# A seven-product unit for one more value/gate column group, its two raw-weight additions done by accumulating transfers

## The chip, the cores and the metric

One Trainium2 chip, one core. The metric is the device time of one execution in microseconds (us), the median of several runs; the profile is one further execution on the same core. PE is TensorE (PEld its weight load), DVE is VectorE, ACT is ScalarE, POOL is GpSimd, SP is SyncE, which issues most loads.

## The reference

Two layers on 256 tokens of width 2048 in float32: a gated linear attention (GLA) layer with 4 heads, then a retention layer with 8 heads, each with a residual add, and a final RMSNorm. Of the GLA layer:

```python
proj = h @ w_in                       # q, k, v, gate
log_a = jax.nn.log_sigmoid(((h @ w_a1) @ w_a2 + b_a)) / 16.0
scores = jnp.einsum('bhtk,bhsk,bhtsk->bhts', qb, kb, decay)   # causal, chunked with a state
o = o * lax.rsqrt(jnp.mean(o * o, axis=-1, keepdims=True) + EPS)
return (o.reshape(B, S, D_INNER) * head_g * jax.nn.silu(gate)) @ w_out
```

A GLA head has 256 key columns and 1024 value columns; the kernel treats its values and gates as two column groups of 512, so head 1 has groups g2 and g3.

## The kernel before

**Precision.** Every large product of float32 matrices is three matmuls of rounded halves: high x high, high x low, low x high. The token side lies split in SBUF (`xhl` for the layer's input, `ogt` for the mixer's output, both transposed). The weight side is split on the way: a *step* is a block of 256 x 512 weights (512 KB). SP loads it into one of eight `raw` buffers, ACT writes its high half `hi` (L298), DVE its low half `lo` (L299), PE multiplies. `hi_p` and `lo_p` have four buffers each, so a step's `hi` can be written when PE has used up a step four places or so before; `LOOK = 3` steps are split ahead.

**Groups and units.** A plain group of 512 output columns is eight steps of 12 matmuls for its values (`gv`, `group_x`) and eight for its gates (`gg`): 192 matmuls. Some pairs of groups are done as a *unit* (`values_and_gates` for heads, `out_pair` for the output projection): the first half of the contraction, as a 2 x 2 block product of tokens by columns, takes seven products of 12 matmuls (P1 to P8 without P4; each product has two steps of 6) in place of eight, and the second half is eight direct steps (v4 to v7, g4 to g7): 84 + 96 = 180 matmuls. A unit needs sums of token blocks (`make_sums`, four tiles, on DVE and ACT) and sums of weight blocks. The latter are made in the `raw` buffers: transfers from DRAM that add to what is there (`accum_op`, issued by POOL, L310), and for P6 two additions of one raw buffer to another on DVE (L293), written in `EARLY = 2` steps ahead. `UNIT` is the order of the steps. `JOINT` lists the units: of the GLA heads only g5 and g7, of the GLA output projection both pairs of its first half (`gae`).

**Head 1.** After its q/k group (`gqk`) come, in the program, the side work of that head, taken up a piece at a time between steps: the decays (`lc`), seven levels of masked scores (`w`, matmuls `lv` of 128 x 128), their masking on DVE (`m`, L819 and L821), fourteen small additions on POOL (`s`, L828), and the split into `sc` (ACT L722, DVE L723). `o_part` multiplies `sc` by the values (`go_ps`); `og_part` normalises (the chain `hm`, `hr_nw`, `hr` of two-element DVE instructions), scales by the gate `gsg`, transposes on PE (`got_tp`) and writes `ogt` (ACT L499, DVE L500). The gate's SiLU, `gsg` (L686), empties the PSUM banks of the gate group.

**Order.** A scheduler fixes each engine's order at build time; every engine then works its list in that order. PSUM has four accumulator banks (`acc`, handed out in turn by `slots`); g3's gates follow g2's in banks that `gsg` of g2 must empty. `rs` is a pool of one 16 KB buffer per partition: first the residual `resid`, loaded at the start, later the token sums `xsum`. Token sums for g5 and g7 (`xsum`) are made during head 2; those for the output pairs (`osum`) during g3.

Of the kernel before, what the change touches and what calls it, by code (L numbers as in the profile page):

```python
# [17 lines left out]
P = 128  # L18
SEQ = 256
D = 2048  # L20
# [44 lines left out]
def _plan():  # L65


    loads, subs = [], []

    def load(gid, j):  # L70
        loads.append((gid, j))
        return len(loads) - 1

    def use(c, pre=None, post=()):
        subs.append((c, pre, post))

    def plain(gid, js=range(NSUB)):
        for j in js:
            use(load(gid, j))

    def pair(g, v, q=None, order=None):
        order = (order or UNIT).split()
        x = [load(g, 0), load(g, 1)] if order[0] == "P1" else []
        z = []
        later = max(("P3", "P6"), key=order.index)
        for n, tok in enumerate(order):
            kind, i = tok[0], tok[1:]
            if kind in "qvg":
                plain({"q": q, "v": v, "g": g}[kind], [int(i)])
            elif tok == "z":  # L90
                z += [load(v, 2), load(v, 3)]
            elif tok == "P2":
                plain(g, [2, 3])
            else:
                if tok == "P1" and not x:
                    x += [load(g, 0), load(g, 1)]
                for j in range(2):
                    post = []
                    if tok == later:
                        post.append((z[j], (v, j)))  # L100
                    if tok == "P1":
                        post.append((x[j], (v, j)))
                    if tok == "P6":
                        post.append((x[j], (g, 2 + j)))
                    use(z[j] if tok in ("P3", "P7") else x[j], z[j] if tok == "P6" else None, post)

    def out_cols_of(name, half, cut, joint):
        for c in (0, 2):
            cols = [(name, half, c + n) for n in range(2)]
            if joint[c // 2]:  # L110
                pair(cols[1], cols[0])
                continue
# [36 lines left out]
    buf = []  # L149
    for c in range(len(loads)):  # L150
        b = min([*range(NRAW), *_spare(loads[c])], key=lambda n: free[n])
        buf.append(b)
        free[b] = last[c]
    return loads, subs, places, last, buf


UNIT = "P1 v4 z P3 v5 P5 v6 P6 P2 v7 P7 g4 g5 P8 g6 g7"
MIXED = "q0 q1 P1 q2 q3 q4 z P5 q5 P6 q6 q7 P2 P3 v4 v5 v6 P7 v7 g4 g5 P8 g6 g7"
WHOLE = " ".join(f"q{j}" for j in range(NSUB)) + " " + UNIT


def ret_order(h):
# [4 lines left out]
HEAD = 4  # L167
EARLY = 2
JOINT = {
    "a": (5, 7),  # L170
    ("ao", 0): (True, True),
    ("ao", 1): (False, True),
    ("ro", 0): (False, True),
# [5 lines left out]
def kernel(  # L179
# [104 lines left out]
    def emit_split(pieces=1, between=None):  # L284
        i = emitted["sub"]
        c, pre, post = subs[i]
        emit_raws(c)
        src = raws[c]
        for n in range(i + 1, min(i + 1 + EARLY, len(subs))):
            at, by = subs[n][:2]  # L290
            if by is not None and n not in added:
                added.add(n)
                nc.vector.tensor_tensor(raws[at], raws[at], raws[by], ALU.add)  # L293
        hi, lo = split_tiles(i)
        step = SUB // pieces
        for k in range(pieces):
            sl = slice(k * step, (k + 1) * step)
            a = nc.scalar.activation(hi[:, sl], src[:, sl], AF.Copy)  # L298
            b = nc.vector.tensor_tensor(lo[:, sl], src[:, sl], hi[:, sl].bitcast(F32), ALU.subtract)  # L299
            if i >= last0 - 4:  # L300
                keep(a)
                keep(b)
            if i == 0:
                first(a, b)
                if k == 0:
                    between()
        splits[i] = (hi, lo)
        emitted["sub"] += 1
        for n, key in post:
            nc.gpsimd.dma_start(raws[n], block(key), accum_op=ALU.add)  # L310
        emit_raws(c)
# [125 lines left out]
    def sums_in_v(name):  # L437
        return lambda n: v_p.tile([P, 2, QK, 2, P], F32R, tag="v", name=f"{name}{n}")

    def make_sums(lhs, name, where):  # L440
        s = cur["s"] = [None] * 4
        room = where(name)
        tt = nc.vector.tensor_tensor
        y = [t4_p.tile([P, QK, SEQ], F32, tag="t4", name=f"{name}_y{i}") for i in range(2)]
# [33 lines left out]
    def get_resid(name):  # L478
        r = rs_p.tile([P, 2, D], F32, tag="rs", name=name)
        nc.gpsimd.dma_start(r, cur["resid_at"])  # L480
        cur["resid"] = r

    def put_resid(name):
        at = dram_p.tile([P, 2, D], F32, tag=name, name=name)
        nc.scalar.dma_start(at, cur["resid"])
# [17 lines left out]

    sm = const([P, 96], "smalls")[:, 0:S_N]
    ident = const([P, P], "ident")
    cur["resid"] = rs_p.tile([P, 2, D], F32, tag="rs", name="resid")
    xhl = const([P, NKT, 2, SEQ], "xhl", F32R)
    ogt = const([P, NKT, 2, SEQ], "ogt", F32R)
    trig = const([P, 2, SEQ], "trig")
# [84 lines left out]
        nc.vector.tensor_scalar(m, ss, 1.0 / D, EPS, ALU.mult, ALU.add)  # L594
        rsqrt(r[:, 0, ts], m, n, name)

    def square_sum(t, c):
        junk = sg_p.tile([P, GW], F32, tag="sg", name="sqj")
        return nc.scalar.activation(
            junk, cur["resid"][:, t, c * GW : (c + 1) * GW], AF.Square, accum_out=ssum[:, t, c : c + 1]  # L600
        )

    zs = sc_p.tile([80, SEQ], F32R, tag="dm", name="zs", bufs=1)
# [38 lines left out]
                make_xhl(kt)  # L642

    def gate_low_rank():
        for t in range(2):
            keep(nc.sync.dma_start(cur["resid"][:, t, :], x_n[:, t, :]))
            yield
        nc.gpsimd.dma_start(mask_t, mask_in)
        for c in range(8):
            square_sum(c // 4, c % 4)  # L650
            if c % 2:
                yield
        token_norm(rr, "n1")
# [181 lines left out]
    def gla_head(h):  # L835
# [70 lines left out]
        def joint_turn(tok):  # L906
            if tok == "v4":
                o_part(0)
            elif tok == "g5":
                o_part(1)  # L910
            else:
                advance()

        for gi in range(2):
# [14 lines left out]
            def v_hook(j):  # L929
                if h > 0 and gi == 1 and j == 1:  # L930
                    o_part(0)
                if h == 1 and gi == 1 and j > 1:
                    if j == 2:
                        cur["making"] = make_sums(ogt, "osum", sums_in_v)
                    if j < 6:
                        next(cur["making"])

            def g_hook(j):
                if h == 0 and gi == 1 and j == 5:
                    o_part(0)  # L940
                if gi == 1 and j == (6 if h == 0 else 2):
                    o_part(1)
                if gi == 1 and h == 1 and j == 3:
                    next(cur["making"])

            if h == 0 and gi == 1:
                drain_side()
                side.append(scores())
            if h == 2 and gi == 0:
                side.append(make_sums(xhl, "xsum", sums_in_rs))  # L950
            pv = group_x(xhl, f"gv{g}", v_hook)
            vs.append(v_evac(pv, r2, f"gv{g}"))
            sgs.append(g_evac(group_x(xhl, f"gg{g}", g_hook), r, f"gsg{g}"))
# [20 lines left out]
            f"xt2_{c}",  # L974
        )

    def out_pair(c, first, name, final=False):
        lhs, s = ogt, cur["s"]
        B, A, C, V1 = acc(4, f"{name}e{c}_ps", which=list(slots))
        slots.rotate(-2)  # L980
# [34 lines left out]
        cur["pin"] = final  # L1015
        product(A, plain(0, 0), stop=True)
        advance()
        direct(lhs, (C, V1), 4)
        join(g, 0, A)
        advance()  # L1020
        product(C, summed(0))
        advance()
        direct(lhs, (C, V1), 5)
        drain_side()
        product(P5, summed(1), stop=True)
        direct(lhs, (C, V1), 6)
        for t in range(2):
            join(c, t, P5)
        product(A, summed(2), stop=True)
        product(B, plain(4, 0))  # L1030
        join(c, 0, A, ALU.subtract)
        direct(lhs, (C, V1), 7, stop=True)
# [55 lines left out]
    def out_half(first, final, name, cut=0, hook=None, joint=(False, False)):  # L1088
        pend = {}
        for c in range(4):  # L1090
            if joint[c // 2]:
                if c % 2 == 0:
                    out_pair(c, first, name)
                continue
            if cut and c == 0:
                if True:
# [346 lines left out]

    for h in range(2):
        gla_head(h)
    slots = deque((2, 3, 0, 1))
    out_half(True, False, "ga", joint=JOINT["ao", 0])
    slots = deque((2, 3, 0, 1))
    put_resid("resid_x")
    for h in range(2, 4):  # L1450
        gla_head(h)
    get_resid("gb_resid")
# [125 lines left out]
```

## Time and profile before

| | |
|---|---|
| median of 3 runs | 1374.77 us (1374.18 to 1375.06) |
| profiled execution | 1373.6 us, span 1371.8 us |
| PE busy | 1361.9 us (99%) |
| DVE, ACT, POOL busy | 1100.0 (80%), 846.6 (62%), 136.7 us (10%) |
| granted TensorE clock | 0.998 |
| DMA | 315.03 MB, mean 230 GB/s |

The times are those of one execution each; the rows of the profile belong to one that took 1373.6 us, of which 1371.8 us lie between its first and last instruction. A row of the order in time begins with start and duration in us.

### The profile page before, as it was taken

How to read it: one execution, taken by the hardware profiler on the slowest of the kernel's cores; microseconds unless marked ns; L12 is line 12 of the kernel's file. 1: busy time of each engine (PE TensorE's matmuls, PEld its weight loads, DVE VectorE, ACT ScalarE, POOL GpSimd, SP SyncE). 2: the span in 40 equal slices, each digit the busy share in tenths (PEclk: the TensorE clock that was granted, in tenths of full speed). 3: DMA queues.
4: the chain of work that ended last, by engine and by line, in shares of the span. 5: the costliest groups of instructions: out<-in, count | busy, mean ns of one | idle time of the engine just before them, and what ended most of it. 6: DMA issues, size and time to landing. Idle time of an engine off the chain costs nothing.

```text
span 1371.8 us, 18375 instructions
## 1 busy us (share of the span) xinstructions
PE 1361.9 (99%) x6564; PEld 1143.5 (83%) x6564; DVE 1100.0 (80%) x1524; ACT 846.6 (62%) x1116; POOL 136.7 (10%) x194
## 2 busy tenths in 40 slices
PE   9999999999999999999999999999999999999997
PEld 8888888888888888888888888888888888888886
DVE  7686795987878896769888888887867897889796
ACT  6576656656567747656666566655546666666565
POOL 1003020110021021001011010100101101010010
PEclk9999999999999999999999999999999999999999
DMA  9755566789658667868897878896798797869773
GB/s 365 257 172 167 174 203 184 158 249 324 192 153 268 205 205 180 314 168 239 271 321 201 256 202 252 207 313 215 174 363 230 234 262 195 262 194 321 236 179 121
DMA packets 84507, 315.03 MB, mean 230 GB/s; under 512 B 9776, under 2 KB 10800, under 8 KB 83136
## 3 DMA queue, kind: packets, MB, share of 16 engines
q1 hardware_dynamic: 67200, 241.63, 50.6%
q0 software_dynamic: 15920, 64.89, 23.7%
q10 hardware_dynamic: 1296, 7.35, 1.5%
q8 instruction: 51, 0.84, 0.2%
q14 instruction: 40, 0.33, 0.1%
HBM read 303.35 MB, written 10.49 MB: 229 GB/s over the span
## 4 chain that ended last, share of the span: by engine, by line
PE 96%; DMA 2%; DVE 1%; issue 1%; ACT 0%; DVEq 0%; POOL 0%; ACTq 0%; POOLq 0%
PE rqk_ps L383 8%; PE re_ps L412 7%; PE re_ps L413 7%; PE re_ps L411 7%; PE rqk_ps L384 4%; PE gqk_ps L383 4%; PE gg_ps L341 3%; PE gv_ps L342 3%; PE gv_ps L341 3%; PE gv_ps L340 3%; PE gg_ps L342 3%; PE gg_ps L340 3%; PE ge_ps L413 2%; PE ge_ps L411 2%; PE ge_ps L412 2%; PE gae_ps L413 2%
## 5 line engine op out<-in xcount | busy, mean ns | idle before, releaser
L299 DVE TENSOR_TENSOR lo<-raw,hi 128x1024 fp32r<-128x1024 f32 (+1 forms) x568 | 687.1, 1219 | 215.6 <-ACT hi L298 206.5
L298 ACT ACTIVATE hi<-raw 128x1024 fp32r<-128x1024 f32 (+1 forms) x568 | 596.1, 1055 | 393.8 <-PE gg_ps L342 49.0
L383 PE MATMUL rqk_ps<-xhl,hi 128*128 128x512 f32 x480 | 162.8, 397 | 0.0
L412 PE MATMUL re_ps<-lo,xhl 128*128 128x512 f32 x352 | 137.4, 390 | 0.3 <-DVE lo L299 0.3
L413 PE MATMUL re_ps<-hi,xhl 128*128 128x512 f32 x352 | 137.1, 390 | 0.0
L310 POOL DMA_DIRECT2D raw<-in_w_all x90 | 78.0, 868 | 555.4 <-DVE lo L299 270.6
L411 PE MATMUL re_ps<-hi,xhl 128*128 128x512 f32 x352 | 132.4, 391 | 0.0
L384 PE MATMUL rqk_ps<-xhl,lo 128*128 128x256 f32 x480 | 122.3, 280 | 0.0
L383 PEld LDWEIGHTS rqk_ps<-xhl,hi 128*128 128x128 f32 x480 | 89.5, 188 | 17.9
L384 PEld LDWEIGHTS rqk_ps<-xhl,lo 128*128 128x128 f32 x480 | 87.5, 189 | 3.4
L412 PEld LDWEIGHTS re_ps<-lo,xhl 128*128 128x128 f32 x352 | 66.1, 188 | 13.9 <-DVE lo L299 0.8
L413 PEld LDWEIGHTS re_ps<-hi,xhl 128*128 128x128 f32 x352 | 66.1, 188 | 13.7
L411 PEld LDWEIGHTS re_ps<-hi,xhl 128*128 128x128 f32 x352 | 66.0, 188 | 13.3
L383 PE MATMUL gqk_ps<-xhl,hi 128*128 128x512 f32 x216 | 76.6, 399 | 0.0
L341 PE MATMUL gg_ps<-lo,xhl 128*128 128x512 f32 x192 | 75.4, 393 | 0.0
L341 PE MATMUL gv_ps<-lo,xhl 128*128 128x512 f32 x192 | 75.2, 392 | 0.0
L340 PE MATMUL gv_ps<-hi,xhl 128*128 128x512 f32 x192 | 75.1, 393 | 0.0
L342 PE MATMUL gv_ps<-hi,xhl 128*128 128x512 f32 x192 | 75.0, 391 | 0.0
L342 PE MATMUL gg_ps<-hi,xhl 128*128 128x512 f32 x192 | 74.9, 390 | 0.0
L340 PE MATMUL gg_ps<-hi,xhl 128*128 128x512 f32 x192 | 74.8, 391 | 0.0
L828 POOL TENSOR_TENSOR s<-s,m 128x64 f32<-128x64 f32 x56 | 36.0, 674 | 232.6 <-DVE m L819 223.3
L384 PE MATMUL gqk_ps<-xhl,lo 128*128 128x256 f32 x216 | 59.0, 280 | 0.0
(434 smaller groups left out, 2654.8 us busy)
## 6 DMA issues: line engine op xcount, KB each, us to landing
raw<-in_w_all SPq DMA_DIRECT2D x449, 512.0 KB, 5.0
raw<-in_w_all POOLq DMA_DIRECT2D x90, 512.0 KB, 6.9
resid<-in_x_n SPq DMA_DIRECT2D x2, 1024.0 KB, 10.0
gg<-in_gn_g POOLq DMA_DIRECT2D x8, 256.0 KB, 4.4
resid_x<-resid ACTq DMA_DIRECT2D x1, 2048.0 KB, 7.9
gb<-in_gn_b POOLq DMA_DIRECT2D x8, 256.0 KB, 5.8
gb_resid<-resid_x POOLq DMA_DIRECT2D x1, 2048.0 KB, 11.1
resid_g<-gb_resid ACTq DMA_DIRECT2D x1, 2048.0 KB, 9.5
```

What stands on the lines that cost most here:

```text
L298: a = nc.scalar.activation(hi[:, sl], src[:, sl], AF.Copy)
L299: b = nc.vector.tensor_tensor(lo[:, sl], src[:, sl], hi[:, sl].bitcast(F32), ALU.subtract)
L310: nc.gpsimd.dma_start(raws[n], block(key), accum_op=ALU.add)
L340: pin(mm(ps, xh, hi[:, q, :], start=kt == begin, stop=False))
L341: pin(mm(ps, xh, lo[:, q, :], start=False, stop=False))
L342: pin(mm(ps, xl, hi[:, q, :], start=False, stop=kt == end - 1))
L383: mm(ps[c], wh, rhs[:, kt, :, :], start=kt == 0, stop=False)
L384: mm(ps[c][:, 0, :], wl, rhs[:, kt, 0, :], start=False, stop=False)
L411: pin(mm(ps, xh, hi[:, q, :], start=start, stop=False, **again))
L412: pin(mm(ps, xh, lo[:, q, :], start=False, stop=False, **again))
L413: pin(mm(ps, xl, hi[:, q, :], start=False, stop=stop, **again))
L828: nc.gpsimd.tensor_tensor(dst, dst, side_of(m[:, li, :], z), ALU.add)
```

## The change

Group g3 becomes a unit too, with the order `UNIT`. Its matmuls go from 192 to 180, its steps from 16 to 22, and it needs six more accumulating loads. What comes with it:

- The two raw-weight additions for its P6 are transfers from one SBUF buffer to another with `accum_op`, issued by POOL; all other units keep the DVE additions.
- The token sums `xsum` are made during head 1's q/k group, kept in DRAM (`keep_sums`, 2 MB) and loaded again before head 2. They lie in the one buffer of `rs`, so the input rows for the norm go into two tiles of the value pool at the start, and the residual is loaded (`get_x`, 2 MB by POOL) after g3's last use of the sums.
- `osum` is made at five places of g3's unit, into `cur["os"]`.
- The first output pair (`gae`, columns 0 and 1) has a new order, `LATE` with `late_direct`: P1, P2, P3 come before the direct step v4, so the first use of g2's and g3's `ogt` is later, and the side work (`og_part`) is spread over it.

```diff
@@ plan and JOINT
-                pair(cols[1], cols[0])
+                pair(cols[1], cols[0], order=LATE if cols[0] == ("ao", 0, 0) else None)
+LATE = "P1 P2 z P3 v4 P5 v5 P6 v6 v7 P7 g4 g5 P8 g6 g7"
-    "a": (5, 7),
+    "a": (3, 5, 7),
@@ emit_split
-                nc.vector.tensor_tensor(raws[at], raws[at], raws[by], ALU.add)
+                if loads[at][0] == ("ag", 3):
+                    nc.gpsimd.dma_start(raws[at], raws[by], accum_op=ALU.add)
+                else:
+                    nc.vector.tensor_tensor(raws[at], raws[at], raws[by], ALU.add)
@@ new
+    def get_x():
+        cur["resid"] = rs_p.tile([P, 2, D], F32, tag="rs", name="resid")
+        for t in range(2):
+            nc.gpsimd.dma_start(cur["resid"][:, t, :], x_n[:, t, :])
@@ gate_low_rank
-            keep(nc.sync.dma_start(cur["resid"][:, t, :], x_n[:, t, :]))
+            xs.append(v_p.tile([P, D], F32, tag="v", name=f"x_n{t}"))
+            keep(nc.sync.dma_start(xs[t], x_n[:, t, :]))
@@ gla_head
             if tok == "v4":
                 o_part(0)
+                if h == 1:
+                    cur["making"] = make_sums(ogt, "osum", sums_in_v, "os")
...
+            elif h == 1 and tok in ("P3", "v5", "P5", "P6", "P8"):
+                next(cur["making"])
...
-            if h == 2 and gi == 0:
-                side.append(make_sums(xhl, "xsum", sums_in_rs))
+            if h == 1 and gi == 0:
+                keep_sums("xsum")
@@ out_pair, first pair of the GLA output
+        if late_direct:
+            product(B, plain(4, 0))
+            join(g, 0, A)
+            advance()
+            product(C, summed(0))
+            while len(side) > 1:
+                advance()
+            advance()
+            direct(lhs, (C, V1), 4)
...
@@ program
     for h in range(2):
         gla_head(h)
+        if h == 0:
+            side.append(make_sums(xhl, "xsum", sums_in_rs))
+    get_x()
+    cur["s"] = cur["os"]
...
     put_resid("resid_x")
+    reload_sums("xsum2")
```

The scheduler moves more than the diff says. On PE, at the start of g3 before (`gv_ps`): the last scores matmul (`w_x` into `lv`) stands 43 matmuls above these rows' first `go_ps`, of which the last eight are shown.

```order
L342 MATMUL gv_ps_1946<-hi_1901,xhl 128x512
L340 MATMUL gv_ps_1947<-hi_1901,xhl 128x512
L341 MATMUL gv_ps_1947<-lo_1902,xhl 128x512
L342 MATMUL gv_ps_1947<-hi_1901,xhl 128x512
L340 MATMUL gv_ps_1946<-hi_1925,xhl 128x512
L341 MATMUL gv_ps_1946<-lo_1926,xhl 128x512
L696 MATMUL go_ps_1984<-gv_1741,sc_1850 128x512
L697 MATMUL go_ps_1984<-gv_1741,sc_1850 128x512
```

The same place of the changed kernel (`ge_ps_1973` takes P1, `ge_ps_1975` takes v4 and P3):

```order
L773 MATMUL lv_1_1641<-w_x 128x128 x2
L415 MATMUL ge_ps_1973<-hi_1924,xhl 128x512
L416 MATMUL ge_ps_1973<-lo_1925,xhl 128x512
L417 MATMUL ge_ps_1973<-hi_1924,xhl 128x512
L415 MATMUL ge_ps_1973<-hi_1924,xhl 128x512
L416 MATMUL ge_ps_1973<-lo_1925,xhl 128x512
L417 MATMUL ge_ps_1973<-hi_1924,xhl 128x512
L707 MATMUL go_ps_2016<-gv_1763,sc_1872 128x512
L708 MATMUL go_ps_2016<-gv_1763,sc_1872 128x512
L707 MATMUL go_ps_2017<-gv_1763,sc_1872 128x512
L708 MATMUL go_ps_2017<-gv_1763,sc_1872 128x512
L415 MATMUL ge_ps_1975<-hi_1947,xhl 128x512
```

Between the last scores matmul and the use of the finished scores `sc` stand six matmuls now. In all, 12 matmuls of P1 and the 8 of levels 4 to 7 stand between the start of g3 and `go_ps`; before, these 8 stood ahead of g3, and 26 matmuls of g3 ahead of `go_ps`.

On ACT, in the changed kernel (`hi_1947` to `hi_1998` are the steps v4, P3 and v5 of g3; `gg_ps` are g2's gate banks, of which `ge_ps_1975` reuses the first):

```order
L302 ACTIVATE hi_1947<-raw_1796 128x1024
L302 ACTIVATE hi_1977<-raw_1825 128x1024
L302 ACTIVATE hi_1987<-raw_1852 128x1024
L302 ACTIVATE hi_1998<-raw_1875 128x1024
L733 ACTIVATE sc_1872<-s_1_1643 128x384
L697 ACT_TABLE_LOAD
L697 ACTIVATE gsg_1967<-gg_ps_1768,rr 128x512
```

Before, the order on ACT was the same (three `hi`, `sc`, table load, `gsg`), but no product of g3's values waited for `gsg`: `gv_ps` of g3 lay in the banks that g2's values had left.

On DVE, at the first output pair. Before, the last of the chain `hr` and the scalings of `go` stand ahead of the pair's steps (`hi_2293` and `hi_2346` are steps of its P1 and of P3):

```order
L496 SCALAR_TENSOR_TENSOR hr_2228<-hr_nw 128x2
L894 SCALAR_TENSOR_TENSOR go_1995<-go_1995,hr_2228,gsg_1943 128x512 x2
L299 TENSOR_TENSOR lo_2294<-raw_2091,hi_2293 128x1024
L299 TENSOR_TENSOR lo_2320<-raw_2109,hi_2319 128x1024
L894 SCALAR_TENSOR_TENSOR go_2199<-go_2199,hr_2228,gsg_2337 128x512 x2
L299 TENSOR_TENSOR lo_2347<-raw_2134,hi_2346 128x1024
L500 SCALAR_TENSOR_TENSOR ogt<-got_tp_2282,smalls,ogt 128x256
```

In the changed kernel (`lo_2503` and `lo_2515` are the two steps of P6, `lo_2527` and `lo_2547` are v6 and v7):

```order
L303 TENSOR_TENSOR lo_2503<-raw_2143,hi_2502 128x1024
L505 SCALAR_TENSOR_TENSOR hr_2353<-hr_nw 128x2
L303 TENSOR_TENSOR lo_2515<-raw_2145,hi_2514 128x1024
L905 SCALAR_TENSOR_TENSOR go_2027<-go_2027,hr_2353,gsg_1967 128x512
L905 SCALAR_TENSOR_TENSOR go_2277<-go_2277,hr_2353,gsg_1971 128x512
L905 SCALAR_TENSOR_TENSOR go_2027<-go_2027,hr_2353,gsg_1967 128x512
L905 SCALAR_TENSOR_TENSOR go_2277<-go_2277,hr_2353,gsg_1971 128x512
L303 TENSOR_TENSOR lo_2527<-raw_2294,hi_2526 128x1024
L998 TENSOR_TENSOR resid<-gae_p_2375,resid 128x512 x2
L303 TENSOR_TENSOR lo_2547<-raw_2312,hi_2546 128x1024
L509 SCALAR_TENSOR_TENSOR ogt<-got_tp_2424,smalls,ogt 128x256
```

The chain `hm` to `hr` and the four scalings now stand between the steps P2 and P6 of the output pair. On PE the products P1, P2, P3, P5 and P6 (60 matmuls) stand ahead of the eight transposes `got_tp` of g2's output, and four matmuls of v4 follow before the first that needs a low half of `ogt`.

More of the change, by code (lines that the diff above doesn't have):

```diff
@@ L438, in sums_in_v, with make_sums @@
         return lambda n: v_p.tile([P, 2, QK, 2, P], F32R, tag="v", name=f"{name}{n}")
-    def make_sums(lhs, name, where):
-        s = cur["s"] = [None] * 4
+    def make_sums(lhs, name, where, into="s"):
+        s = cur[into] = [None] * 4
         room = where(name)
@@ L505 @@
     ident = const([P, P], "ident")
-    cur["resid"] = rs_p.tile([P, 2, D], F32, tag="rs", name="resid")
     xhl = const([P, NKT, 2, SEQ], "xhl", F32R)
@@ L595, in token_norm, with square_sum @@
         rsqrt(r[:, 0, ts], m, n, name)
-    def square_sum(t, c):
+    def square_sum(t, c, src=None):
         junk = sg_p.tile([P, GW], F32, tag="sg", name="sqj")
+        src = cur["resid"][:, t] if src is None else src
         return nc.scalar.activation(
-            junk, cur["resid"][:, t, c * GW : (c + 1) * GW], AF.Square, accum_out=ssum[:, t, c : c + 1]
+            junk, src[:, c * GW : (c + 1) * GW], AF.Square, accum_out=ssum[:, t, c : c + 1]
         )
@@ L644, in gate_low_rank @@
     def gate_low_rank():
+        xs = []
         for t in range(2):
[L646 removed]
+            xs.append(v_p.tile([P, D], F32, tag="v", name=f"x_n{t}"))
+            keep(nc.sync.dma_start(xs[t], x_n[:, t, :]))
             yield
@@ L649, in gate_low_rank @@
         for c in range(8):
-            square_sum(c // 4, c % 4)
+            square_sum(c // 4, c % 4, xs[c // 4])
             if c % 2:
@@ L931, in v_hook @@
                     o_part(0)
[L932 to L936, printed above, removed]
             def g_hook(j):
@@ L942, in g_hook @@
                     o_part(1)
-                if gi == 1 and h == 1 and j == 3:
-                    next(cur["making"])
             if h == 0 and gi == 1:
@@ L975, in out_transposes, with out_pair @@
         )
-    def out_pair(c, first, name, final=False):
+    def out_pair(c, first, name, final=False, late_direct=False):
         lhs, s = ogt, cur["s"]
@@ L1017, in out_pair @@
         advance()
[L1018 to L1032, printed above, removed]
+        if late_direct:
[7 more added lines that the diff above has]
+            direct(lhs, (C, V1), 4)
+            advance()
+            product(P5, summed(1), stop=True)
+            advance()
+            direct(lhs, (C, V1), 5)
+            for t in range(2):
+                join(c, t, P5)
+            drain_side()
+            product(A, summed(2), stop=True)
+            direct(lhs, (C, V1), 6)
+            join(c, 0, A, ALU.subtract)
+            direct(lhs, (C, V1), 7, stop=True)
+        else:
+            direct(lhs, (C, V1), 4)
+            join(g, 0, A)
+            advance()
+            product(C, summed(0))
+            advance()
+            direct(lhs, (C, V1), 5)
+            drain_side()
+            product(P5, summed(1), stop=True)
+            direct(lhs, (C, V1), 6)
+            for t in range(2):
+                join(c, t, P5)
+            product(A, summed(2), stop=True)
+            product(B, plain(4, 0))
+            join(c, 0, A, ALU.subtract)
+            direct(lhs, (C, V1), 7, stop=True)
         product(A, summed(3), stop=True)
@@ L1092, in out_half @@
                 if c % 2 == 0:
-                    out_pair(c, first, name)
+                    out_pair(c, first, name, late_direct=first and c == 0 and name == "ga")
                 continue
```

## The prediction

> **What bounds the kernel now.** I read the engine totals first, then what PE waited for, then the windows around the third to fifth column groups, then each engine's order in time there.
>
> ```profile
> span 1371.8 us, 18375 instructions
> PE 1361.9 (99%) x6564; PEld 1143.5 (83%) x6564; DVE 1100.0 (80%) x1524; ACT 846.6 (62%) x1116; POOL 136.7 (10%) x194
> ```
>
> ```profile
> PE warm_ps L520 <- POOL lnone L522: 1.0, 1, 1.0
> PE re_ps L412 <- DVE lo L299: 0.3, 1, 0.3
> PE zps L639 <- DVE wa L613: 0.3, 1, 0.3
> ```
>
> The second view is the whole list of PE's waits: 1.6 us in three places. So a matmul that goes is a gain in full, and a microsecond of a new wait is a loss in full: PE has nowhere to make it up. The question is whether the engines that feed PE keep their lead at the two places that the change reorders. The windows are q/k and values/gates of g2, g3, and the first output pair; columns are PE, PEld, DVE, ACT, POOL.
>
> ```profile
> 125.00:153.00 28.00, 28.00 (x157) 24.12 (x156) 17.20 (x33) 18.63 (x32) 0.00 (x0) 1.00 0.49 156
> 153.00:201.00 48.00, 48.00 (x236) 40.51 (x235) 40.45 (x71) 27.91 (x38) 6.83 (x11) 1.00 0.65 201
> 201.00:249.00 48.00, 48.00 (x214) 39.72 (x213) 29.99 (x43) 29.08 (x40) 3.98 (x7) 1.00 0.60 168
> 249.00:290.00 41.00, 41.00 (x190) 34.06 (x189) 36.00 (x40) 27.01 (x32) 5.17 (x6) 1.00 0.83 241
> ```
>
> DVE is at 84% in g2 and 88% in the output pair, with PE at 100%: what DVE gets there in addition comes late.
>
> **Matmuls saved.** PE's order in time at the end of g2, and from the chain the scores matmuls:
>
> ```profile
> 198.23 0.39 PE L340 MATMUL gg_ps<-hi,xhl 128*128 128x512 f32 x1
> ...
> 200.95 0.39 PE L340 MATMUL gv_ps<-hi,xhl 128*128 128x512 f32 x1
> ```
>
> ```profile
> 195.91 1.34 PE lv L762 x12
> ```
>
> Twelve matmuls lie between the starts 198.23 and 200.95: 2.72 us, 0.227 each. The unit has 180 in place of 192, so 12 x 0.227 = 2.7 us go. A small scores matmul costs 1.34/12 = 0.11.
>
> **First wait: the scores at the start of g3.** Count from g3's first matmul as zero. By the order, P1's 12 matmuls and 8 small ones come first: PE is at `go_ps` at 12 x 0.227 + 8 x 0.11 = 3.6 and, after four of them, at v4 at 4.5. Both wait for ACT: `go_ps` for `sc`, v4 for the bank that g2's `gsg` empties. What feeds them, on ACT (a step of g2, then the end of its scores), on DVE (two pieces of `w`, then a `lo` and `m`) and on POOL (the additions of head 1 in one block, and those of head 2 in two):
>
> ```profile
> 194.41 1.06 ACT L298 ACTIVATE hi<-raw 128x1024 fp32r<-128x1024 f32 x1 [2.12 <-PE gg_ps L342]
> ```
>
> ```profile
> 203.21 0.53 ACT L722 ACTIVATE sc<-s 128x384 fp32r<-128x384 f32 x1 [1.00 <-POOL s L828]
> 203.76 1.28 ACT L686 ACT_TABLE_LOAD   x1
> 205.05 1.27 ACT L686 ACTIVATE gsg<-gg_ps,rr 128x512 f32<-128x512 f32 x2
> ```
>
> ```profile
> 190.75 0.42 DVE L800 TENSOR_TENSOR w<-w,qk 128x256 f32<-128x256 f32 x1
> 191.08 0.41 DVE L801 TENSOR_TENSOR w<-w,qk 128x256 f32<-128x256 f32 x1
> ```
>
> ```profile
> 192.76 1.22 DVE L299 TENSOR_TENSOR lo<-raw,hi 128x1024 fp32r<-128x1024 f32 x1
> 193.90 0.68 DVE L819 TENSOR_TENSOR m<-lv,mask 128x512 f32<-128x512 f32 x1
> ```
>
> ```profile
> 194.73 8.45 POOL L828 TENSOR_TENSOR s<-s,m 128x64 f32<-128x64 f32 x14 [32.77 <-DVE m L819]
> ```
>
> ```profile
> 377.20 4.73 POOL L828 TENSOR_TENSOR s<-s,m 128x64 f32<-128x64 f32 x8 [69.51 <-DVE m L819]
> 386.59 3.21 POOL L828 TENSOR_TENSOR s<-s,m 128x64 f32<-128x64 f32 x6 [4.66 <-DVE m L821]
> ```
>
> Before, the additions began at 194.73, 6.2 us ahead of g3's first matmul (200.95), and `sc` had its high half at 203.74. Now `m` stands in DVE's queue behind the `lo` of P1 and of v4. The first row of ACT shows that a `hi` starts when PE has used up the step whose buffer it takes. P1's first `hi` takes that of g2's fifth gate step, used up three steps and the 8 small matmuls before the last one drains at zero: -(3 x 2.72 + 0.9) + 0.16 = -8.9 (0.16 is 0.39 less 0.23). With 1.06 and 1.22 its `lo` ends at -6.6. Behind it come 13 pieces of `w` (0.33 from start to start), a `lo` (1.14 likewise, 192.76 to 193.90), 4 pieces, the `lo` of v4, and `m`: 17 x 0.33 + 2 x 1.14 + 0.68 = 8.6, so 2.0. POOL follows 0.15 later (194.73 against 193.90 + 0.68) and takes 4.73 + 3.21 = 7.9: 10.1. From the start of `sc` to the first of two `gsg` ends 205.05 + 0.64 - 203.21 = 2.5: 12.6. PE stood ready at 4.5: **a wait of 8.1 us**, first at `go_ps`, then at v4. Bounds: with DVE free throughout, `m` still needs v4's `hi`, whose buffer is free at -2.72 + 0.16; that gives -2.56 + 1.06 + 1.22 + 0.68 = 0.4 for `m`, 11.0 for `gsg`, a wait of 6.5. With one more `lo` ahead of `m` and the block of 8.45 in place of 7.9 it is 9.8. I take 8.1, since DVE's queue is in order and full (84%).
>
> **The rest of g3: the adding transfers.** A transfer between two SBUF buffers is not in the trace. The nearest row is the accumulating load of the same 512 KB on the same queue:
>
> ```profile
> L310 POOL DMA_DIRECT2D raw<-in_w_all x90: 843/862/1024, 243.2 to 1326.9; - x90
> ```
>
> ```profile
> DMA to landing us min/median/max: 5.2/6.9/14.3
> ```
>
> Count from v4's first matmul. The second transfer waits for the `lo` of P5's second step; its `hi` takes v4's buffer, used up 23 matmuls on (5.2 + 0.16), so it and the `lo` end at about 7.7. Landing at 6.9 gives 14.6, and `hi` and `lo` of P6's second step end at 14.6 + 1.06 + 1.22 = 16.9. PE comes for them after 72 matmuls, 16.3: 0.6 us late. With 5.2 nothing is late, with 14.3 it is 8.0. I take 0.6, as the DMA engines are only 0.60 busy in g3's window. [...] The two DVE additions saved are 2 x 1.22 us, on an engine that is not then the last to finish, so nothing.
>
> **Second wait: the first output pair.** Rows of DVE from head 1's end, of before, and PE's P6:
>
> ```profile
> 237.84 0.15 DVE L886 TENSOR_TENSOR hm<-sso 128x2 f32<-128x2 f32 x1
> 238.03 0.17 DVE L887 TENSOR_SCALAR hm<-hm 128x2 f32<-128x2 f32 x1
> ...
> 243.21 1.42 DVE L894 SCALAR_TENSOR_TENSOR go<-go,hr,gsg 128x512 f32<-128x512 f32 x2
> ...
> 257.78 1.22 DVE L293 TENSOR_TENSOR raw<-raw,raw 128x1024 f32<-128x1024 f32 x1
> 258.92 1.22 DVE L299 TENSOR_TENSOR lo<-raw,hi 128x1024 fp32r<-128x1024 f32 x1
> 260.05 0.47 DVE L500 SCALAR_TENSOR_TENSOR ogt<-got_tp,smalls,ogt 128x256 fp32r<-128x256 f32 x1
> ...
> 263.11 2.35 DVE L299 TENSOR_TENSOR lo<-raw,hi 128x1024 fp32r<-128x1024 f32 x2
> ...
> 266.96 1.28 DVE L990 TENSOR_TENSOR resid<-gae_p,resid 128x512 f32<-128x512 f32 x2
> ```
>
> ```profile
> 267.01 0.39 PE L411 MATMUL gae_ps<-hi,osum 128*128 128x512 f32 x1
> ```
>
> Count from the pair's first matmul. PE has 60 matmuls, 8 transposes and 4 matmuls before it needs the first low half of `ogt`: 64 x 0.227 + 0.9 = 15.4. DVE comes to that row through 12 `lo` (1.14), two raw additions (1.14), 13 two-element instructions (0.19 apart), three joins to `resid` (0.64), four scalings (0.71) and the low half (0.4): 13.7 + 2.3 + 2.5 + 1.9 + 2.8 + 0.4 = 23.6. It starts on them at about 0.8, since `osum` and the last gate addition stand ahead. So the low half is there at 24.4, **9.0 us late**, part of it already at P6, whose `lo` stand behind the chain. Lower bound: before, this stretch of DVE was as full, and P6's `lo` (263.11 + 1.14) was 2.9 ahead of its matmul (267.01 + 0.23); new in it are the chain, the scalings and the gate addition, 2.5 + 2.8 + 0.7 = 6.0, so at least 3.1. Upper: 10.5, with `lo` at 1.22. I take 9.0, as it follows from the order.
>
> **Edits costed at nothing.** Six more steps are 6 x 1.06 on ACT and 6 x 1.22 = 7.3 on DVE, and five additions in g3's evacuation 3.4: 30.0 + 10.7 of 45 us in g3, hidden but for the order. `xsum` (about 8 us of DVE) goes into the q/k window, where 17.2 of 28 us are used; uncovered, it would cost what exceeds the 10.8 left, nothing. The residual's load has its last reader of `xsum` 69 matmuls (15.6 us) ahead of the pair and its first join some 8 us into it; the nearest load is this one:
>
> ```profile
> gb_resid<-resid_x POOLq DMA_DIRECT2D x1, 2048.0 KB, 11.1
> ```
>
> 11.1 us lie inside 23. The reload of `xsum` has 70 us until g5. If the residual came late, each us would be PE's.
>
> **The sum.** 1373.6 - 2.7 + 8.1 + 0.6 + 9.0 = 1388.6 for a run like the profiled one; the median of the runs shown is 1.2 above it: **1390 us** (1389.8).
>
> **Rivals.**
> - *Only the scores wait (chance 0.2).* DVE's stretch in the output pair hides the chain, as it hid all of its work before without a wait of PE. 1374.8 - 2.7 + 8.1 + 0.6 = 1380.8. Against it: the scalings must end before the transposes, and the order puts nine `lo` in front of them.
> - *The adding transfers are slow (0.12).* They land like the slowest, 14.3, while the pair's loads run: 8.0 in place of 0.6, 1397.2. For it: new traffic on one queue. Against: 0.60 busy. [...]
> - *No wait (0.05): faster.* The unit gives its 2.7 us and the scores come in time: 1372.1. It decides where POOL's fourteen additions begin: 8.1 us earlier than worked out, at -6.0, about where they began before (-6.2). Against: v4's buffer is not free before -2.56, and `m` stands behind it.
> - That the unit is not shorter is excluded: the order has 12 matmuls fewer.
>
> **How the numbers follow.** The forecast has 0.63. A measurement tells 0.2% (2.7 us) from no change; the third rival's gain lies on that edge, so half of it is faster, half the same, and all else is slower. The range takes the lower bounds together, 1374.8 - 2.7 + 6.5 + 3.1 = 1381.7, and the first rival, so 1380; at the top the slow transfers with little more, 1399 (all upper bounds together: 1400.4).
>
> **What would show it.** In the changed profile, PE's list of waits should have `go_ps` and the first `ge_ps` of v4 released by ACT (`sc`, `gsg`), some 8 us together, POOL's additions ending about 10 us after P1's first matmul, and `gae` waiting for DVE (`lo`, `ogt`), some 9 us. P6's `hi` should wait for the adding transfer by a microsecond at most on PE's side. If PE still waits less than 3 us in all, I am wrong on the order; if `gae` shows no wait, on the chain; if the transfer lands after 10 us or under 5, on that term.

## The result, and the profile after

The changed kernel took 1393.86 us (median of 4 runs, 1391.38 to 1394.61) beside 1374.91 us of the kernel before on the same chip: a ratio of 1.0135, 95% interval 1.0119 to 1.0151, slower by 19 us. The forecast was 1390, with a range from 1380 to 1399. The profiled execution took 1391.38 us, the lowest of the four; its span is 17.8 us longer than that of before. First its totals, then the larger entries of the list of PE's waits (us in total, times, longest):

```profile
span 1389.6 us, 18411 instructions
PE 1366.6 (98%) x6552; PEld 1142.6 (82%) x6552; DVE 1108.6 (80%) x1535; ACT 854.0 (61%) x1126; POOL 146.6 (11%) x206
```

```profile
PE go_ps L707 <- ACT sc L733: 7.1, 1, 7.1
PE gae_ps L416 <- DVE lo L303: 1.9, 1, 1.9
PE go_ps L707 <- ACT gv L1412: 1.1, 1, 1.1
PE gae_ps L417 <- DVE ogt L509: 1.0, 1, 1.0
...
PE gae_ps L415 <- ACT hi L302: 0.9, 2, 0.7
```

PE stands idle 1389.6 - 1366.6 = 23.0 us, before 9.9: 13.1 more, at the two places of the forecast. But it is also busy 4.7 us longer with 12 matmuls (2.7 us) fewer, so 7.4 us went into matmuls that took longer. Where the time went, by place: PE's matmuls at the start of the first output pair and at the start of head 2's q/k, first of before, then of after.

```profile
248.56 0.38 PE L706 MATMUL got_tp<-ident,go 128*128 128x128 f32 x2
...
330.03 1.07 PE L383 MATMUL gqk_ps<-xhl,hi 128*128 128x512 f32 x4
```

```profile
257.53 0.47 PE L415 MATMUL gae_ps<-hi,ogt 128*128 128x512 f32 x1 [0.15 <-ACT go_ps L885]
...
347.90 1.07 PE L387 MATMUL gqk_ps<-xhl,hi 128*128 128x512 f32 x4
```

The unit ends 9.0 us later than g3 did; the output pairs take 90.4 us in place of 81.5, 8.9 more. That is the whole 17.9; behind the pairs nothing more is lost.

The first place, in order of time: DVE's `m`, POOL's additions, ACT's `sc` and `gsg`, and PE.

```profile
200.55 0.69 DVE L830 TENSOR_TENSOR m<-lv,mask 128x512 f32<-128x512 f32 x1 [0.78 <-PE lv L773]
```

```profile
201.39 9.26 POOL L839 TENSOR_TENSOR s<-s,m 128x64 f32<-128x64 f32 x14 [2.92 <-DVE m L830]
```

```profile
210.69 0.52 ACT L733 ACTIVATE sc<-s 128x384 fp32r<-128x384 f32 x1 [5.45 <-POOL s L839]
211.23 1.28 ACT L697 ACT_TABLE_LOAD   x1
212.52 1.26 ACT L697 ACTIVATE gsg<-gg_ps,rr 128x512 f32<-128x512 f32 x2
```

```profile
199.45 0.39 PE L415 MATMUL ge_ps<-hi,xhl 128*128 128x512 f32 x1
...
211.26 0.79 PE L707 MATMUL go_ps<-gv,sc 128*128 128x512 f32 x1 [7.11 <-ACT sc L733]
...
213.27 0.79 PE L415 MATMUL ge_ps<-hi,xhl 128*128 128x512 f32 x1
```

The four `go_ps` matmuls behind the wait take 2.0 us, not 0.9: TensorE's granted clock is halved there. Windows of 3.41 us around both places (behind the window's length PE's busy time; the last three numbers are granted clock, DMA share and GB/s):

```profile
205.51:208.93 3.42, 0.00 (x0) 0.00 (x0) 3.31 (x4) 0.00 (x0) 3.42 (x4) 1.00 0.04 14
208.93:212.34 3.41, 1.08 (x3) 0.89 (x4) 1.65 (x3) 1.64 (x2) 1.73 (x7) 0.50 0.49 154
212.34:215.75 3.41, 3.41 (x9) 2.27 (x8) 0.71 (x2) 1.92 (x4) 0.00 (x0) 0.50 0.00 0
270.37:273.78 3.41, 1.53 (x7) 1.06 (x7) 3.41 (x6) 1.06 (x1) 1.77 (x2) 1.00 0.82 126
273.78:277.19 3.41, 3.41 (x12) 2.73 (x11) 3.41 (x5) 1.74 (x2) 0.85 (x1) 0.50 1.02 251
```

The clock falls to half at 208.9, in the middle of the wait, and again at 273.8, after a window in which PE stood for 1.9 of 3.4 us; it comes back one full window of work later. Work at half clock fills 211.26 to 215.75 and 273.78 to 277.19, 7.9 us, so 4.0 us are lost. The other 3.4 of the 7.4 lie between matmuls: behind each of the ten waits that before did not have a matmul starts without the overlap of its forerunner (0.39 less 0.23, 0.16 us each, an estimate of 1.6), and the rest is in gaps that the list of waits does not name.

The second place, DVE's chain to `hr` and the scalings in the first output pair:

```profile
258.43 0.16 DVE L897 TENSOR_TENSOR hm<-sso 128x2 f32<-128x2 f32 x1
...
272.36 0.15 DVE L505 SCALAR_TENSOR_TENSOR hr<-hr_nw 128x2 f32<-128x2 f32 x1
...
273.58 2.73 DVE L905 SCALAR_TENSOR_TENSOR go<-go,hr,gsg 128x512 f32<-128x512 f32 x4
```

Thirteen instructions of 0.16 us take from 258.43 to 272.51, since eight `lo`, two raw additions and a join stand between them; before, they took from 237.84 to the scalings at 243.21. From 262.53 to 277.53, where PE's longest waits of the pair lie, DVE has no idle time (15.0 of 15.0 us busy).

### The profile page after: what moved, and what is told of

The parts are those of the page before. It is cut to its first block, busy times and chain, and to the rows that moved or that the text cites. A ratio compares the mean times of both kernels' runs of the same rounds, so it can differ in the third digit from the quotient of the medians.

```text
span 1389.6 us, 18411 instructions
## 1 busy us (share of the span) xinstructions
PE 1366.6 (98%) x6552; PEld 1142.6 (82%) x6552; DVE 1108.6 (80%) x1535; ACT 854.0 (61%) x1126; POOL 146.6 (11%) x206
## 4 chain that ended last, share of the span: by engine, by line
PE 93%; DMA 2%; DVE 2%; issue 1%; ACT 1%; POOL 1%; SPq 0%; DVEq 0%; POOLq 0%; ACTq 0%
PE rqk_ps L387 8%; PE re_ps L415 8%; PE re_ps L416 8%; PE re_ps L417 8%; PE rqk_ps L388 4%; PE gqk_ps L387 4%; PE ge_ps L415 3%; PE ge_ps L416 3%; PE ge_ps L417 3%; PE gg_ps L345 3%; PE gv_ps L345 3%; PE gv_ps L344 3%; PE gv_ps L346 3%; PE gg_ps L344 3%; PE gg_ps L346 3%; DMA raw<-in_w_all 2%
## 5 line engine op out<-in xcount | busy, mean ns | idle before, releaser
L303 DVE TENSOR_TENSOR lo<-raw,hi 128x1024 fp32r<-128x1024 f32 (+1 forms) x574 | 694.4, 1220 | 223.2 <-ACT hi L302 212.0
L314 POOL DMA_DIRECT2D raw<-in_w_all x96 | 83.1, 872 | 570.6 <-DVE lo L303 324.6
L387 PEld LDWEIGHTS rqk_ps<-xhl,hi 128*128 128x128 f32 x480 | 89.5, 188 | 17.9
L345 PE MATMUL gg_ps<-lo,xhl 128*128 128x512 f32 x160 | 62.9, 393 | 0.0
L345 PE MATMUL gv_ps<-lo,xhl 128*128 128x512 f32 x160 | 62.7, 392 | 0.0
L344 PE MATMUL gv_ps<-hi,xhl 128*128 128x512 f32 x160 | 62.7, 394 | 0.0
L346 PE MATMUL gv_ps<-hi,xhl 128*128 128x512 f32 x160 | 62.6, 391 | 0.0
L346 PE MATMUL gg_ps<-hi,xhl 128*128 128x512 f32 x160 | 62.3, 389 | 0.0
L344 PE MATMUL gg_ps<-hi,xhl 128*128 128x512 f32 x160 | 62.3, 391 | 0.0
```

The lines of the kernel that those rows point to most:

```text
L344: pin(mm(ps, xh, hi[:, q, :], start=kt == begin, stop=False))
L345: pin(mm(ps, xh, lo[:, q, :], start=False, stop=False))
L346: pin(mm(ps, xl, hi[:, q, :], start=False, stop=kt == end - 1))
L387: mm(ps[c], wh, rhs[:, kt, :, :], start=kt == 0, stop=False)
```

## The experiments

Ratios are to the kernel before on the same chip, with 95% intervals; one per mille is 1.4 us.

### The raw additions on DVE again

```diff
-if loads[at][0] == ("ag", 3):
+if False:
     nc.gpsimd.dma_start(raws[at], raws[by], accum_op=ALU.add)
```

> The changed kernel, but g3's two additions of raw weights are again made by DVE (1.22 us each) and not by adding transfers. Theory (two chains come late at PE: the scores at the start of g3, and hr with the scalings in the first output pair; the adding transfers are covered): no difference, ratio to before 1.0135 within 0.002, the wait at go_ps 7 us as before and the clock halved behind it. Rival (the adding transfers and what waits behind them on POOL's queue carry part of the loss): 2 to 4 us faster, ratio 1.011 or less. Other rival (DVE is the scarce engine in g3): 2.4 us slower, ratio 1.0153.

Measured: 1390.39 us, ratio 1.0115 (1.0098 to 1.0132). The wait at `go_ps` for `sc` (7.1) is the same, those in the pair are nearly so (4.2 us for 4.8), and the wait of 1.1 us for `gv` is gone. The profiled execution was at half clock in g3 for longer: its granted clock was 0.82, 0.50 and 0.50 in the first three of the windows above, where the changed kernel has 1.00, 0.50 and 0.50. The time is 2.7 us less than the changed kernel's, but the intervals overlap: this run alone does not decide between the theory and the first rival. The transfers themselves, in the changed kernel:

```profile
L295 POOL DMA_DIRECT2D raw<-raw x2: 862/872/882, 220.2 to 222.6; - x2
...
DMA to landing us min/median/max: 4.4/4.7/5.1
```

### Adding transfers in the units of the kernel before

```diff
-nc.vector.tensor_tensor(raws[at], raws[at], raws[by], ALU.add)
+if loads[at][0] in (("ag", 5), ("ag", 7)):
+    nc.gpsimd.dma_start(raws[at], raws[by], accum_op=ALU.add)
+else:
+    nc.vector.tensor_tensor(raws[at], raws[at], raws[by], ALU.add)
```

> The kernel before, with the raw additions of its units g5 and g7 (four of 512 KB) done by adding transfers between buffers on POOL's queue in place of DVE. Theory (they land in 4.4 to 5.1 us beside the loads and are covered; DVE is not scarce there): no difference, ratio 1.000 within 0.002, no wait of PE in g5 or g7. Rival (they hold up POOL's accumulating loads or P6's hi): PE waits for a hi in those units, 1 to 4 us, ratio 1.001 to 1.003.

Measured: 1381.6 us, ratio 1.0055 (1.0042 to 1.0067): four adding transfers cost 7.6 us, more than the rival had. PE's new waits, the time from issue to landing, and ACT's `hi` behind g5's second transfer:

```profile
PE ge_ps L414 <- ACT hi L301: 2.5, 2, 1.9
PE ge_ps L415 <- DVE lo L302: 1.5, 2, 0.8
```

```profile
DMA to landing us min/median/max: 4.4/6.0/8.7
```

```profile
423.59 1.06 ACT L301 ACTIVATE hi<-raw 128x1024 fp32r<-128x1024 f32 x1 [4.62 <-DMA raw<-raw]
```

An addition of 1.22 us became an issue of 0.86 and 4.4 to 8.7 us to landing, on the path from P5's `lo` to P6's `hi`. The theory fell: in units that run without other waits the transfers are not covered. The waits are 4.0 us of the 7.6; the mean granted clock of the profiled execution was 0.997, beside 0.998 before. The transfers are also no light traffic. The page's third part for before (loads on q1, accumulating ones on q0), then q0 of this run:

```profile
q1 hardware_dynamic: 67200, 241.63, 50.6%
q0 software_dynamic: 15920, 64.89, 23.7%
```

```profile
q0 software_dynamic: 16496, 66.99, 24.4%
```

As estimates from these shares: q1's 241.63 MB are 461 times 512 KB, so a plain load takes 0.506 x 1371.8 / 461 = 1.5 us of all 16 engines; q0's 64.89 MB, most of them accumulating loads, took 2.6 us for each 512 KB; the four adding transfers took 0.244 x 1380.3 - 0.237 x 1371.8 = 11.7 us, 2.9 each.

### The moves without the unit

```diff
-"a": (3, 5, 7),
+"a": (5, 7),
...
-pair(cols[1], cols[0], order=LATE if cols[0] == ("ao", 0, 0) else None)
+pair(cols[1], cols[0], order=None)
```

The places where `osum` is made and the pair's order of products are set back too.

> The changed kernel without the unit itself: g3 with plain 16 steps again, the first output pair in the order of before, osum in g3's hooks as before; only xsum made in head 1's q/k, kept in DRAM and reloaded, and the residual loaded late. Theory (xsum and the residual cost nothing): ratio 1.000 within 0.002. Rival (the transfers of 2 MB each, or xsum's DVE work, hold up something): 1.002 to 1.005.

Measured: 1374.17 us, ratio 1.0001 (0.9992 to 1.0010). Making `xsum` early, keeping it and loading the residual late cost nothing, as costed.

### The scores' product later

```diff
-if tok == "v4":
+if tok == ("v5" if h == 1 else "v4"):
     o_part(0)
...
+keep(nc.scalar.activation(hw["sc"][:, 0, :], src, AF.Copy))   # in o_part, behind gsg
...
-mm(ps[t], ah, v[:, s, 0, :], start=n == 0, stop=False)
+pin(mm(ps[t], ah, v[:, s, 0, :], start=n == 0, stop=False))
```

> The changed kernel, but g2's output product go_ps stands after v5 in place of v4's head in PE's order, and sc is issued on ACT behind g2's gsg, so that neither go_ps nor v4's bank waits for the scores. Theory: the wait of 7.1 us goes, and so does the stretch of 6.8 us at half clock, 4.6 us of it with work (2.3 us lost): 9.4 us, ratio to before 1.0067. Rival (PE waits there for something else just behind, the loads or DVE): the wait moves to v4, P3 or P5 and less than 3 us come back, ratio over 1.011.

Measured: 1388.76 us, ratio 1.0107 (1.0092 to 1.0122): the wait for `sc` is gone, and 3.8 of the 9.4 us came back. PE waits a little later instead, for a `lo` that stands in DVE's queue behind an `osum_f` (L460) whose buffer POOL's additions still read:

```profile
210.82 0.69 DVE L460 TENSOR_TENSOR osum_f<-osum_y 128x512 f32<-128x512 f32 x1 [1.90 <-POOL s L839]
```

```profile
216.17 0.80 PE L416 MATMUL ge_ps<-lo,xhl 128*128 128x512 f32 x1 [2.88 <-DVE lo L303]
```

The clock halved there too: from 216.17 to 219.21 matmuls start 0.43 us apart, not 0.23. The next edit takes that wait away; `osum`'s pieces are also taken up later, at v6, P6, P2, P7 and P8:

```diff
+if into == "os":
+    tt = lambda *x: keep(nc.vector.tensor_tensor(*x))
```

> As the run with go_ps behind v5 (ratio 1.0107), and osum's additions held behind sc in DVE's program order: in that run DVE stood 1.9 us at an osum_f that waits for POOL's additions (its buffer is m's), with three lo behind it, and PE then waited 2.9 us for a lo. Theory (that blocked queue is what PE waits for): 2.9 us and the 3.4 us at half clock behind them (1.7 lost) go, ratio 1.0073. Rival (DVE has too much work in g3 whatever its order): the wait moves on, ratio over 1.009.

Measured: 1386.16 us, ratio 1.0090 (1.0076 to 1.0104). The wait of 2.9 and the halved clock in g3 are gone; 2 us of small waits stay there, 0.3 to 0.9 each. Both readings hold in part: the queue was what PE waited for, and half of the 4.6 us moved on (the intervals of the two runs overlap, so the waits say this more surely than the times). POOL's additions also got shorter, now that no `osum` addition stands beside them on DVE; they took 9.3 us in the changed kernel and in the run before this one:

```profile
201.58 8.01 POOL L841 TENSOR_TENSOR s<-s,m 128x64 f32<-128x64 f32 x14 [2.92 <-DVE m L832]
```

### Without that wait, the raw additions on DVE again

The two edits before, and the first experiment's.

> The run with osum behind sc (ratio 1.0090, scores no longer in PE's way), with g3's two raw additions on DVE again in place of adding transfers. Theory (in the changed kernel the wait for the scores covered the transfers; without it they cost what they cost g5 and g7 of the kernel before, 7.6 us for two units, 3.8 us each): ratio 1.0062. Rival (in g3 they are covered anyway; DVE, full in the first output pair, pays for two more additions): ratio 1.009 or more.

Measured: 1381.81 us, ratio 1.0060 (1.0047 to 1.0072), as the theory had it: 4.1 us less than the run before. PE has no wait in g3 at all now; what is left stands in the pair:

```profile
PE gae_ps L417 <- DVE ogt L511: 2.1, 1, 2.1
PE gae_ps L415 <- ACT hi L302: 1.9, 1, 1.9
PE gae_p L416 <- DVE lo L303: 1.4, 1, 1.4
```

So the transfers cost 4 us once the scores are out of the way (3.8 in the units of before). That the wait for `sc` had covered them in the changed kernel is not shown: it ended at 211.26, and they were issued at 220.2 and 222.6. There they met DMA engines that had been idle (share 0.00 from 212.34 to 219.16) and landed in 4.4 and 5.1 us; in the run before this one they took 4.4 and 7.5, and in g5 and g7 of the kernel before 4.4 to 8.7, where the page of that run has the DMA engines at 0.9 or more (414 to 449 us) and at 0.7 or more (518 to 552).

The unit itself now gains: PE's first matmul of the output pair starts at 247.04, 1.5 us earlier than g3 ended before, and the whole loss lies in the output pairs.

### Plain columns behind the unit

```diff
-("ao", 0): (True, True),
+("ao", 0): (False, True),
```

> The run with osum behind sc and DVE's additions (ratio 1.0060, no wait of PE in g3), with the first two output columns as plain columns of 16 steps and 192 matmuls in place of the pair with 180: the unit stays in g3, its 2.7 us are given back. Theory (what is left of the loss is that the pair's five products, 1.36 us of PE for 1.14 us of DVE in each step, stand in front and hr, the scalings and the joins don't fit beside them; plain steps take 2.72 us of PE for the same 1.14): no wait there, ratio 1.000, at most 1.002. Rival (head 1's outputs come too late after a unit whatever follows): PE waits for ogt before the ninth k tile, ratio over 1.003.

Measured: 1376.08 us, ratio 1.0018 (1.0009 to 1.0027), the end of the theory's range. PE's new waits there are two:

```profile
PE ga_ps L344 <- ACT ogt L510: 0.6, 1, 0.6
PE ga_ps L346 <- DVE ogt L511: 0.6, 1, 0.6
```

The pair's waits go, and with them 5.8 us in spite of 12 more matmuls. The late outputs of head 1 by themselves cost only 1.2 us of waits here, so the loss of the second place is the pair behind the unit. That it is the five products in front, with DVE at 1.14 of each 1.36 us, fits a DVE without idle time there; but this run takes away the pair's raw additions and accumulating loads as well, and does not tell them apart.

### The chain to `hr` held together

```diff
+if cur.get("chain"):
+    keep(b)
...
-nc.vector.tensor_tensor(m, sso[:, :, 0], sso[:, :, 1], ALU.add)
+pin(nc.vector.tensor_tensor(m, sso[:, :, 0], sso[:, :, 1], ALU.add))
```

> The changed kernel, but in the first output pair DVE's 13 two-element instructions hm to hr are held together in program order with lo, so that no lo stands between them; scalings and transposes then come earlier. Theory: the pair's waits (4.8 us listed) and its 3.4 us at half clock (1.7 us lost), with about 1 us of matmul starts after waits, go: 7.5 us, ratio 1.008. Rival (DVE is full there whatever its order; lo comes late instead): PE waits for lo in P2, P3 or P5 and less than 2 us come back, ratio over 1.012.

Measured: 1391.33 us, ratio 1.0128 (1.0113 to 1.0143), the rival's. The chain took 2.5 us (258.19 to 260.72), the transposes came 11 us earlier (264.86, not 276.27), and the pair's waits for `lo` and `ogt` shrank to 0.2 us each. In their place came a later one, for an accumulating load:

```profile
288.06 2.95 ACT L302 ACTIVATE hi<-raw 128x1024 fp32r<-128x1024 f32 x3 [5.85 <-DMA raw<-in_w_all]
```

PE waited 3.2 us behind it. With the transposes early, P5 and P6 stand later in PE's order, which would also hold up the accumulating loads behind them (argued from the order, not tested); behind the wait, from 290.11 to 296.28, matmuls run at half clock, 0.43 us from start to start. The same edit on the run with `osum` behind `sc`:

> The run with osum behind sc and, besides, hr's 13 small instructions held together in the first output pair. Theory (both losses are orders, and the loads were late in the pair only because g3 had held their buffers): PE's waits of both places go, the unit's 2.7 us less of matmuls show, ratio 0.998 to 1.002. Rival (the pair is short of DMA: in the run with hr together a hi waited 5.9 us for an accumulating load, PE 3.2 us behind it): a wait for hi of some 3 us and a stretch at half clock stay, ratio 1.004 to 1.007.

Measured: 1387.7 us, ratio 1.0097 (1.0084 to 1.0111): no gain on 1.0090, and slower than the rival's own range. The waits in the pair are 3.8 for a `lo` and 2.6 for a `hi`.

### The wait filled with matmuls

```diff
+for n in range(28):
+    keep(mm(junk, xhl[:, n % 8, 0, 0:P], xhl[:, n % 8], start=True, stop=True))
```

> The changed kernel with 28 more matmuls of 512 columns (28 x 0.227 = 6.4 us) between P1 and go_ps of g3, into a bank that nobody reads. Theory (PE's clock halves because PE stood idle): the granted clock stays at full speed there, the wait shrinks to under 1 us, the start of go_ps does not move, and 2.3 us come back, ratio 1.0118. Rival (the halved clock has another cause, load or time): the clock halves all the same, ratio 1.0135 or more.

Measured: 1395.03 us, ratio 1.0153 (1.0138 to 1.0168). The clock stayed at full speed, the same windows as above:

```profile
205.51:208.93 3.42, 3.42 (x17) 2.84 (x16) 3.20 (x3) 0.00 (x0) 3.42 (x5) 1.00 0.04 17
...
212.34:215.75 3.41, 2.58 (x11) 2.15 (x12) 0.61 (x2) 1.83 (x4) 0.00 (x0) 1.00 0.00 0
```

So in the changed kernel it halved because PE stood idle there: 0.00 us busy of the window ahead, 3.42 here. But no time came back: PE waited 4.5 us later in g3, at 243.04, for a `hi` whose load landed late.

```profile
241.93 2.95 ACT L302 ACTIVATE hi<-raw 128x1024 fp32r<-128x1024 f32 x3 [6.69 <-DMA raw<-in_w_all]
```

The DMA engines stand idle before it (share 0.00 in the last window above). A reading that no run tests is that the steps hold all the buffers, so that the loads can't make up what PE gains. Two of the first four matmuls of `go_ps` also stand behind v4 in this run's order, which was not meant to change.

### `osum` on POOL

```diff
+tt = lambda *x: keep(nc.gpsimd.tensor_tensor(*x))
```

The run changed is the one with ratio 1.0060; `osum`'s subtractions stay on DVE, and its pieces are taken up at P5, v6, P6, P7 and P8.

> The run before with osum's six additions made by POOL (idle there) in place of DVE, 4.8 us of DVE's time between the two places. Theory (DVE's backlog into the first output pair is what is left of the loss): PE's waits for lo, hi and ogt in the pair shrink by 2 to 5 us, ratio 1.003 to 1.005. Rival (the pair's own order, hr between lo, is what is left): no change to the run before within 0.0015, ratio about 1.006.

Measured: 1380.94 us, ratio 1.0050 (1.0037 to 1.0064), between the two forecasts and not told apart from 1.0060. The pair's waits fell from 6.4 to 2.4 us, but PE waited 3.3 us in g3 for `lo`, which took DVE 2.6 times as long (9.54 us for three, the first 5.10) while POOL added:

```profile
219.26 5.06 POOL L449 TENSOR_TENSOR osum_y<-ogt 128x1024 f32<-128x1024 f32 x2
```

```profile
220.31 9.54 DVE L303 TENSOR_TENSOR lo<-raw,hi 128x1024 fp32r<-128x1024 f32 x3 [1.90 <-ACT hi L302]
```

With the chain to `hr` held together as well:

> The run with osum on POOL and hr's 13 instructions held together. Theory (DVE now has room, so the earlier transposes help): the pair's waits go, ratio 0.999 to 1.002. Rival (with hr together P5 and P6 come late in PE's order and their accumulating loads with them, as in the two runs with hr together): a wait of 3 us for a hi stays with a stretch at half clock, ratio 1.004 to 1.007.

Measured: 1384.71 us, ratio 1.0081 (1.0069 to 1.0094): slower than without the edit, and beyond the rival's range. In the two other pairs of runs holding the chain together made no difference clear of noise (1.0128 beside 1.0135, 1.0097 beside 1.0090). No version here beat the kernel before.

## Why the prediction was right, point by point

- **Matmuls saved, -2.7.** Right: 12 fewer.
- **The scores, +8.1.** The place and the releaser were right, the make-up was not. `m` began 1.1 us after P1's first matmul (worked out: 2.0), but POOL's additions took 9.3 us, not 7.9, so `sc` came at 11.2 and not at 10.1. What made them longer was not in the working: `osum`'s additions on DVE beside them (8.0 us where these stand behind `sc`). PE waited 7.1 at `go_ps`, from 4.7 on. The further wait of v4 for `gsg` did not show: four `go_ps` at half clock covered it. At the unit's end 9.0 us were lost; 8.1 and 0.6 less 2.7 were forecast, 6.0.
- **The adding transfers, +0.6.** Priced at the wrong place. In the changed kernel they landed in 4.4 and 5.1 us, not 6.9, the shorter under the 5 that was named as a sign against this term, and PE did not wait for P6. What they held up stands behind P6: the accumulating loads behind them on POOL's queue were issued at 225.1 and 228.6, with the additions on DVE at 223.1 and 225.5, and PE's wait of 1.1 us for `gv` is there only with the transfers. Their cost in the changed kernel is not measured clear of noise (2.7 us, intervals that overlap). With no wait for the scores they cost 3.8 to 4.1 us a unit (two comparisons), within the 0 to 8.0 of the bounds. The second rival had their mechanism, not its size. That two DVE additions saved are worth nothing stands: no run with them on DVE was slower than its fellow without.
- **The first output pair, +9.0.** The place cost 8.9 us, but only 4.8 of it as waits; 1.7 went to the halved clock, 2.4 to starts and gaps. The wait shows first at P6's `hi` and `lo`, as said, and 1.0 us at the low half of `ogt`. The rival in which only the scores wait is refuted. The reason is better told so: behind the unit, a pair with five products in front leaves DVE no room (15.0 of 15.0 us busy; waits of 2.4 in place of 6.4 us when POOL makes `osum`; none of the pair's waits with plain columns). Two of this term's bounds do not come out of its own working: with `lo` and raw additions at 1.22 the upper one is 10.1, not 10.5 (all upper bounds together 1400.0), and P6's `lo` was 3.0 ahead of its matmul, not 2.9. Neither moves the forecast.
- **Left out: the halved clock.** 4.0 us, and 3.4 in starts and gaps, 7.4 together; the waits were forecast 4.6 us too long (17.7 against 13.1). The two errors nearly cancel, and that is luck: the places were foreseen, but the sum of 1388.6 for a run that took 1391.4 is nearer than its terms.
- **Edits at nothing.** For `xsum`, its reload and the late residual confirmed within 0.001 by the run without the unit. The work of six more steps and five more additions was not tested by itself.

## What to carry to other kernels

When an engine that has no slack gets several new waits, taking one away gives back less than its price: the next one shows, here scores, then DVE's queue, then transfers, then loads (3.8 of 9.4 us came back when the wait for `sc` went). Price each alone by a run that has the others removed. A unit that saves matmuls but packs more preparation into the same time pays only where the preparing engines have room; here g3 gained 1.5 us once its waits were gone, and the pair behind it lost more. An idle TensorE can be paid twice, once as a wait and once at half clock after it (here 7.1 us, then 4.5 us of work at a granted clock of 0.50).

## What the runs showed of the hardware that was not expected

- The granted clock changed at steps of 3.41 us: in the changed kernel the stretches at half clock inside the run lasted 6.83 and 3.41 us, and the one at full clock between them 58.03, 17 times 3.41. There the windows with 3.4, 2.3 and 1.9 us without a matmul were each followed by one at half clock; all others, with up to 1.4 us, were followed by one at full clock. So the clock halved even behind a window with 1.5 us of work in it.
- An adding transfer of 512 KB between two buffers took 2.9 us of all 16 DMA engines (the estimate above), twice a plain load (1.5), and 4.4 to 8.7 us to land: 4.4 and 5.1 in the changed kernel, behind DMA engines at a share of 0.00, up to 8.7 in g5 and g7 of the kernel before.
- While POOL made `osum`'s additions of two SBUF operands (219.26 to 232.72 in the run with `osum` on POOL), three `lo` on DVE took 9.5 us together (the first 5.1) in place of 1.22 each, and DVE's `osum` additions went with longer ones on POOL (9.3 in place of 8.0 us for fourteen).
